# RMSNorm with every row written twice: stores and loads in batches of three and two, wide instructions, gamma spread by a matmul

## The chip, the core and the metric

The kernel runs on one core of a Trainium2 chip. The metric is the device time of one execution in microseconds (us). A core has several engines that work side by side, each through its own instructions in order: TensorE (PE, matrix products), VectorE (DVE), ScalarE (ACT), GpSimd (POOL) and SyncE (SP), which here only issues transfers. Sixteen DMA engines move data between the large memory outside the core (DRAM) and the core's own memory, which has 128 partitions. A second memory on the core, PSUM, also has 128 partitions.

## What is computed

```python
"x": (8, 512, 2048) float32, "gamma": (2048,) float32

x_rep = np.repeat(x, 2, axis=1)
rms = np.sqrt((x_rep ** 2).mean(axis=-1, keepdims=True) + 1e-6)
x_norm = x_rep / rms
return (x_norm * gamma[None, None, :]).astype(np.float32)
```

Each of the 4096 rows of 2048 numbers is divided by its root mean square, multiplied by gamma, and written to the output twice in a row. The input has 33.6 MB, the output 67.1 MB.

## The kernel before

The rows are cut into eight tiles of 512 rows: 128 partitions with four rows each (K = 4). A tile has one buffer `y` of eight rows per partition, as wide as its output. A load (L52) puts the four rows of x into its upper half, rows 4 to 7; the result of row k goes to row 2k and its repetition to row 2k + 1, so that the buffer at the end is the output tile in order and a store (L56) writes it out. Three such buffers take turns (`rows`, bufs=3), so a load of tile i waits until the store of tile i - 3 is complete.

For each row, `square` lets ACT square 2048 numbers into PSUM (`sq`, thrown away) and sum them on the way (L64), then take the root of the mean plus 1e-6 (L68). `scale` takes the reciprocal on DVE (L73) and multiplies the row by it and by gamma in one SCALAR_TENSOR_TENSOR (L74). `repeat` copies the result (L80): on ACT for all rows of a part but the last, where DVE does it. `compute` strings these together so that ACT squares row k + 1 while DVE scales row k.

All loads and stores are issued by SyncE, on one queue, in program order, and SyncE waits at each for what it needs. The order is written by hand (`tc.manual_schedule()`): load 0 in two halves, loads 1 and 2, stores 0 and 1, loads 3 and 4, stores 2 and 3, loads 5 and 6, stores 4 and 5, load 7 in two halves, store 6, and store 7 in two halves. Gamma comes in four pieces to one partition, issued by ACT (L98), and is spread over the partitions by GpSimd (L101) into `gamma_b`. L131 and L142 are the start and end of the launch.

Of the kernel before, what the change touches and what calls it, by code (L numbers as in the profile page):

```python
# [1 line left out]

# [4 lines left out]


@with_exitstack
def kernel(  # L10
    ctx: ExitStack,
    tc: tile.TileContext,
    x: bass.AP,
    gamma: bass.AP,
    out: bass.AP,
):
    nc = tc.nc
    P = nc.NUM_PARTITIONS
    f32 = mybir.dt.float32
    Act = mybir.ActivationFunctionType  # L20
    Alu = mybir.AluOpType

    B, S, D = x.shape
    Bo, So, Do = out.shape
    R = So // S
    assert R == 2 and D == Do and B == Bo and So == S * R
    eps = 1e-6
    inv_d = 1.0 / float(D)


    K = 4
    N = B * S
    assert N % (P * K) == 0
    ntiles = N // (P * K)
    x_t = x.rearrange("b s d -> (b s) d").rearrange("(n p k) d -> n p k d", p=P, k=K)
    out_t = out.rearrange("b s d -> (b s) d").rearrange("(n p j) d -> n p (j d)", p=P, j=K * R)

    singles = ctx.enter_context(tc.tile_pool(name="singles", bufs=1))
    rows = ctx.enter_context(tc.tile_pool(name="rows", bufs=3))
    junk = ctx.enter_context(tc.tile_pool(name="junk", bufs=1, space=bass.MemoryType.PSUM))  # L40
    small = ctx.enter_context(tc.tile_pool(name="small", bufs=8))

    ys = []

    def load(i, eng, parts=1):


        y = rows.tile([P, K * R, D], f32, name="y")
        step = K // parts
        for k in range(0, K, step):  # L50
            at = K * (R - 1) + k
            eng.dma_start(out=y[:, at : at + step, :], in_=x_t[i, :, k : k + step, :])  # L52
        ys.append(y)

    def store(i, k0, k1):
        nc.sync.dma_start(  # L56
            out=out_t[i, :, R * k0 * D : R * k1 * D],
            in_=ys[i][:, R * k0 : R * k1, :].rearrange("p j d -> p (j d)"),
        )

    def square(i, k):
        sq = junk.tile([P, D], f32, name="sq")
        ss = small.tile([P, 1], f32, name="ss")
        nc.scalar.activation(  # L64
            out=sq[:], in_=ys[i][:, K * (R - 1) + k, :], func=Act.Square, accum_out=ss[:]
        )
        rms = small.tile([P, 1], f32, name="rms")
        nc.scalar.activation(out=rms[:], in_=ss[:], func=Act.Sqrt, scale=inv_d, bias=eps_t[:])  # L68
        return rms

    def scale(i, k, rms):
        rstd = small.tile([P, 1], f32, name="rstd")
        nc.vector.reciprocal(out=rstd[:], in_=rms[:])  # L73
        nc.vector.scalar_tensor_tensor(  # L74
            out=ys[i][:, R * k, :], in0=ys[i][:, K * (R - 1) + k, :], scalar=rstd[:], in1=gamma_b[:],
            op0=Alu.mult, op1=Alu.mult,
        )

    def repeat(i, k, copy):
        copy(out=ys[i][:, R * k + 1, :], in_=ys[i][:, R * k, :])  # L80

    def compute(i, k0, k1):

        rms = square(i, k0)
        for k in range(k0, k1):
            scale(i, k, rms)
            if k + 1 < k1:
                rms = square(i, k + 1)
                repeat(i, k, nc.scalar.copy)
            else:  # L90
                repeat(i, k, nc.vector.tensor_copy)


    ctx.enter_context(tc.manual_schedule())
    load(0, nc.sync, parts=2)
    gamma_b = singles.tile([P, D], f32, name="gamma_b")
    for c in range(0, D, D // 4):
        nc.scalar.dma_start(  # L98
            out=gamma_b[0:1, c : c + D // 4], in_=gamma[c : c + D // 4].partition_broadcast(1)
        )  # L100
    nc.gpsimd.partition_broadcast(out_ap=gamma_b[:], in_ap=gamma_b[0:1, :])  # L101
    eps_t = singles.tile([P, 1], f32, name="eps_t")
    nc.vector.memset(eps_t, eps)  # L103
    load(1, nc.sync)
    load(2, nc.sync)

    for i in range(ntiles):
        parts = 2 if i == ntiles - 1 else 1
        for k in range(0, K, K // parts):
            compute(i, k, k + K // parts)  # L110
            store(i, k, k + K // parts)

        if i % 2 == 1:
            for j in (i + 2, i + 3):
                if j < ntiles:
                    load(j, nc.sync, parts=2 if j + 1 == ntiles else 1)


# [1 line left out]
_INS = ['x', 'gamma']  # L120
_OUTS = [((8, 1024, 2048), 'float32')]


# [23 lines left out]
```

## Time and profile before

| | |
|---|---|
| median of 4 runs | 239.87 us (239.53 to 240.31) |
| profiled execution | 239.79 us |
| its span, first to last instruction | 238.0 us |
| DVE busy | 90.8 us (38% of the span), 74 instructions |
| ACT busy | 115.3 us (48%), 121 instructions |
| POOL busy | 2.5 us, 5 instructions |
| loads of 4 MB / 2 MB, issue to landing (median) | 25.1 / 9.6 us |
| stores, issue to landing (median) | 26.8 us (4 MB), 31.6 us (8 MB) |

The groups of instructions that matter, as line, engine, operation, what it writes and reads, shape, count, then busy time and mean duration of one in ns, then the idle time of the engine before them and what ended it:

```profile
L64 ACT ACTIVATE sq<-y 128x2048 f32<-128x2048 f32 x32 | 59.9, 1871 | 84.9 <-DMA y<-in_x_dram 84.9
L74 DVE SCALAR_TENSOR_TENSOR y<-y,rstd,gamma_b 128x2048 f32<-128x2048 f32 x32 | 75.3, 2352 | 1.2 <-DVE rstd L73 0.2
L73 DVE RECIPROCAL rstd<-rms 128x1 f32<-128x1 f32 x32 | 5.2, 162 | 115.7 <-ACT rms L68 115.7
L80 ACT COPY y<-y 128x2048 f32<-128x2048 f32 x23 | 43.4, 1888 | 3.7 <-DVE y L74 3.7
L80 DVE COPY y<-y 128x2048 f32<-128x2048 f32 x9 | 11.0, 1226 | 0.3
L68 ACT ACTIVATE rms<-ss,eps_t 128x1 f32<-128x1 f32 x32 | 9.4, 294 | 1.0
L64 ACT ACTIVATION_READ_ACCUMULATOR sq<-y 128x1 f32 x32 | 6.0, 186 | 0.0
L101 POOL PARTITION_BROADCAST gamma_b<-gamma_b x1 | 2.3, 2292 | 8.4 <-DMA gamma_b<-in_gamma_dram 8.4
```

A long idle time says where an engine waited: ACT waited 84.9 us for loads, DVE 115.7 us for ACT, most of it while ACT itself waited.

### The profile page before, as it was taken

To read this page: it belongs to the slowest core of one execution; us is meant where nothing else is said; L and a number is where in the kernel's file an instruction comes from. 1 tells how busy PE (TensorE), PEld (TensorE's weight loads), DVE (VectorE), ACT (ScalarE), POOL (GpSimd) and SP (SyncE) were. 2 spreads that over 40 slices of the span, in tenths; PEclk is the share of its full clock that TensorE was granted. 3 is DMA by queue.
4 is the path that set the end of the run, shared out by engine and by line. 5 is a ranking of instruction groups with operands and counts; after the bars stand their busy time and mean duration, and the time that the engine had idled before them with its cause. 6 is when DMAs were issued, how large, how long until landed. Compare 5 with 4: busy or idle time off the path is not lost.

```text
span 238.0 us, 301 instructions
## 1 busy us (share of the span) xinstructions
DVE 90.8 (38%) x74; ACT 115.3 (48%) x121; POOL 2.5 (1%) x5
## 2 busy tenths in 40 slices
DVE  0086977864000084967000007696600009900000
ACT  2699999990000299997000049999500049700000
POOL 0300000000000000000000000000000000000000
DMA  7999998989899999989898999989898999999996
GB/s 265 430 452 441 441 441 352 529 352 529 352 424 413 435 419 425 529 352 529 352 529 347 441 430 425 474 374 507 352 529 352 402 435 485 441 419 397 424 441 259
DMA packets 2747, 100.69 MB, mean 423 GB/s; under 512 B 309, under 2 KB 309, under 8 KB 313
## 3 DMA queue, kind: packets, MB, share of 16 engines
q1 hardware_dynamic: 2736, 100.66, 98.7%
q14 instruction: 3, 0.02, 0.0%
q10 hardware_dynamic: 8, 0.01, 0.0%
HBM read 33.56 MB, written 67.11 MB: 423 GB/s over the span
## 4 chain that ended last, share of the span: by engine, by line
DMA 66%; ACT 15%; DVE 6%; issue 1%; SPq 0%; DVEq 0%
DMA out_dram<-y 40%; DMA y<-in_x_dram 25%; ACT sq L64 7%; ACT y L80 5%; DVE y L74 5%; ACT rms L68 1%; ACT L68 1%; DVE y L80 1%; DVE rstd L73 0%; SPq L52 0%; DVEq L74 0%; SPq L56 0%
## 5 line engine op out<-in xcount | busy, mean ns | idle before, releaser
L64 ACT ACTIVATE sq<-y 128x2048 f32<-128x2048 f32 x32 | 59.9, 1871 | 84.9 <-DMA y<-in_x_dram 84.9
L74 DVE SCALAR_TENSOR_TENSOR y<-y,rstd,gamma_b 128x2048 f32<-128x2048 f32 x32 | 75.3, 2352 | 1.2 <-DVE rstd L73 0.2
L73 DVE RECIPROCAL rstd<-rms 128x1 f32<-128x1 f32 x32 | 5.2, 162 | 115.7 <-ACT rms L68 115.7
L80 ACT COPY y<-y 128x2048 f32<-128x2048 f32 x23 | 43.4, 1888 | 3.7 <-DVE y L74 3.7
L80 DVE COPY y<-y 128x2048 f32<-128x2048 f32 x9 | 11.0, 1226 | 0.3
L68 ACT ACTIVATE rms<-ss,eps_t 128x1 f32<-128x1 f32 x32 | 9.4, 294 | 1.0
L64 ACT ACTIVATION_READ_ACCUMULATOR sq<-y 128x1 f32 x32 | 6.0, 186 | 0.0
L101 POOL PARTITION_BROADCAST gamma_b<-gamma_b x1 | 2.3, 2292 | 8.4 <-DMA gamma_b<-in_gamma_dram 8.4
L64 ACT ACT_TABLE_LOAD x1 | 1.3, 1283 | 2.1 <-issue 2.1
L68 ACT ACT_TABLE_LOAD x1 | 1.3, 1283 | 0.0
L103 DVE MEMSET eps_t<- 128x1 f32 x1 | 0.1, 59 | 0.8 <-PEq L131 0.8
L131 POOL MEMSET const-float32-0.0<- 128x1 f32 x1 | 0.1, 100 | 0.2 <-issue 0.2
L131 POOL MEMSET const-bfloat16-1.0<- 128x1 bf16 x1 | 0.1, 102 | 0.0
L131 POOL MEMSET const-uint8-127<- 128x1 uint8 x1 | 0.1, 101 | 0.0
L131 POOL MEMSET const-float32-1.0<- 128x1 f32 x1 | 0.1, 98 | 0.0
## 6 DMA issues: line engine op xcount, KB each, us to landing
y<-in_x_dram SPq DMA_DIRECT2D x6, 4096.0 KB, 25.1
y<-in_x_dram SPq DMA_DIRECT2D x4, 2048.0 KB, 9.6
out_dram<-y SPq DMA_DIRECT2D x2, 4096.0 KB, 26.8
out_dram<-y SPq DMA_DIRECT2D x7, 31.6
gamma_b<-in_gamma_dram ACTq DMA_DIRECT2D x4, 2.0 KB
```

Of the source, the lines that this page charges most:

```text
L64: nc.scalar.activation(out=sq[:], in_=ys[i][:, K * (R - 1) + k, :], func=Act.Square, accum_out=ss[:])
L68: nc.scalar.activation(out=rms[:], in_=ss[:], func=Act.Sqrt, scale=inv_d, bias=eps_t[:])
L73: nc.vector.reciprocal(out=rstd[:], in_=rms[:])
L74: nc.vector.scalar_tensor_tensor(out=ys[i][:, R * k, :], in0=ys[i][:, K * (R - 1) + k, :], scalar=rstd[:], in1=gamma_b[:], op0=Alu.mult, o ...
L80: copy(out=ys[i][:, R * k + 1, :], in_=ys[i][:, R * k, :])
L101: nc.gpsimd.partition_broadcast(out_ap=gamma_b[:], in_ap=gamma_b[0:1, :])
L103: nc.vector.memset(eps_t, eps)
L131: nc = _bacc.Bacc("TRN2", target_bir_lowering=False, num_devices=1)
```

## The change

SyncE's order becomes: the first half of load 0, six pieces of gamma, the second half of load 0, the last piece of gamma, loads 1 and 2, stores 0, 1, 2, loads 3, 4, 5, stores 3 and 4, loads 6 and 7, stores 5, 6, 7. Every store is a whole tile, and so is every load but the first.

Gamma goes to one partition (`gamma_row`). Four matmuls with a row of ones spread it over 128 partitions into PSUM, where `gamma_b` now lies.

The work of a tile is done in wide instructions, and not each tile alike. `by_rows` (tiles 0 and 3) sums each row as before, takes root and reciprocal of two rows at once (`root_quick`), scales row by row and copies several rows in one instruction. `sums` and `mixed` (tiles 1, 2, 4, 6, 7) square the rows from `by_row` on in one ACT instruction, into the still unused rows of the output buffer, and sum them in one DVE reduction (`reduce`); the rows before `by_row` are summed as before. `root` raises the mean plus 1e-6 to the power -0.5 on GpSimd for four rows at once. `mixed` puts the squares of the next tile (`ahead`) before its own scaling. The copies are all on DVE (tiles 0, 4), half on ACT and half on DVE (1, 2, 3, 7), or all on ACT (6). In tile 5 ACT scales by the root, DVE multiplies all four rows by gamma in one instruction, and GpSimd makes the copy. The activation table is loaded ahead of the first load.

```diff
-    def store(i, k0, k1):
+    def load(i, k0, k1):
         nc.sync.dma_start(
+            out=ys[i][:, K * (R - 1) + k0 : K * (R - 1) + k1, :], in_=x_t[i, :, k0:k1, :]
+        )
+    def store(i):
+        nc.sync.dma_start(out=out_t[i], in_=ys[i].rearrange("p j d -> p (j d)"))
+    def total(i, k, ss):
+        sq = junk.tile([P, D], f32, name="sq")
+        nc.scalar.activation(
+            out=sq[:], in_=ys[i][:, x_at + k, :], func=Act.Square, accum_out=ss[:, k : k + 1]
+        )
+    def square(i, k0, k1):
+        nc.scalar.activation(
+            out=ys[i][:, k0:k1, :], in_=ys[i][:, x_at + k0 : x_at + k1, :], func=Act.Square
+        )
+    def reduce(i, k0, k1, ss):
+        nc.vector.tensor_reduce(
+            out=ss[:, k0:k1], in_=ys[i][:, k0:k1, :], op=Alu.add, axis=mybir.AxisListType.X
+        )
+    def root(k0, k1, ss):
+        at = ss[:, k0:k1]
+        nc.gpsimd.tensor_scalar(
+            out=at, in0=at, scalar1=inv_d, scalar2=eps, op0=Alu.mult, op1=Alu.add
+        )
+        nc.gpsimd.tensor_tensor(out=at, in0=at, in1=power_t[:, k0:k1], op=Alu.pow)
...
+    gamma_b = junk.tile([P, D], f32, name="gamma_b")
+    cuts = [0, *range(D // 4, D + 1, D // 8)]
...
+    nc.scalar.preload_act_table(Act.Sqrt)
+    load(0, 0, H)
+    for c0, c1 in zip(cuts[:-2], cuts[1:-1]):
+        gamma_piece(c0, c1)
+    load(0, H, K)
+    gamma_piece(cuts[-2], cuts[-1])
+    bank = 512
+    for c0 in range(0, D, bank):
+        nc.tensor.matmul(
+            gamma_b[:, c0 : c0 + bank], ones[:], gamma_row[:, c0 : c0 + bank], start=True, stop=True
+        )
+    load(1, 0, K)
+    load(2, 0, K)
+    def root_quick(k0, k1, ss):
+        at = ss[:, k0:k1]
+        nc.scalar.activation(out=at, in_=at, func=Act.Sqrt, scale=inv_d, bias=eps_t[:])
+        nc.vector.reciprocal(out=at, in_=at)
+    def by_rows(i, copies):
+        ss = [columns() for _ in range(R)]
+        for h, k0 in enumerate(range(0, K, H)):
+            for k in range(k0, k0 + H):
+                total(i, k, ss[h])
+            root_quick(k0, k0 + H, ss[h])
+            scale(i, k0, k0 + H, ss[h])
+        for k0, k1, copy in copies:
+            repeat(i, k0, k1, copy)
+        store(i)
+    def sums(i, by_row):
+        ss = columns()
+        square(i, by_row, K)
+        for k in range(by_row):
+            total(i, k, ss)
+        return i, by_row, ss
+    def mixed(given, copies, ahead=None):
+        i, by_row, ss = given
+        reduce(i, by_row, K, ss)
+        root(0, K, ss)
+        if ahead is not None:
+            ahead = sums(*ahead)
+        scale(i, 0, K, ss)
+        for k0, k1, copy in copies:
+            repeat(i, k0, k1, copy)
+        store(i)
+        return ahead
+    whole = ((0, K, nc.vector.tensor_copy),)
+    shared = ((0, H, nc.scalar.copy), (H, K, nc.vector.tensor_copy))
+    by_scalar = ((0, H, nc.scalar.copy), (H, K, nc.scalar.copy))
+    by_rows(0, whole)
+    two = mixed(sums(1, 1), shared, ahead=(2, 1))
+    mixed(two, shared)
+    for j in (3, 4, 5):
+        new_tile()
+        load(j, 0, K)
+    by_rows(3, shared)
+    _, _, ss = mixed(sums(4, H), whole, ahead=(5, 0))
+    for j in (6, 7):
+        new_tile()
+        load(j, 0, K)
+    reduce(5, 0, K, ss)
+    root(0, K, ss)
+    for k in range(K):
+        nc.scalar.activation(
+            out=ys[5][:, R * k, :], in_=ys[5][:, x_at + k, :], func=Act.Copy, scale=ss[:, k : k + 1]
+        )
+    y_r = ys[5].rearrange("p (k r) d -> p k r d", r=R)
+    nc.vector.tensor_tensor(
+        out=y_r[:, :, 0, :], in0=y_r[:, :, 0, :],
+        in1=gamma_b[:].rearrange("p (k d) -> p k d", k=1).to_broadcast([P, K, D]), op=Alu.mult,
+    )
+    repeat(5, 0, K, nc.gpsimd.tensor_copy)
+    store(5)
+    last = mixed(sums(6, 1), by_scalar, ahead=(7, 0))
+    mixed(last, shared)
```

`load` of before, with its parts, and the functions `square`, `scale`, `repeat` and `compute` in their old form go. `scale` still multiplies a row by its scalar and gamma, now for rows k0 to k1; `repeat` copies rows k0 to k1 in one instruction.

## The prediction

> **What bounds the kernel now.** I read the page's queue table first, then the stretches, the chain that ended last, and last the timeline of one tile.
>
> ```profile
> q1 hardware_dynamic: 2736, 100.66, 98.7%
> HBM read 33.56 MB, written 67.11 MB: 423 GB/s over the span
> ```
>
> The reader is to see 98.7%: the packets of SyncE's one queue fill 16 DMA engines for all but 3.1 us of the 238.0 us span. The rest is nearly all at the two ends:
>
> ```profile
> core 0: us, DVE busy (x) ACT busy (x) POOL busy (x), PEclk, DMA share, GB/s
> 0.00:2.00 2.00, 0.06 (x1) 0.00 (x0) 0.19 (x4) 1.00 0.52 99
> 2.00:30.00 28.00, 14.40 (x13) 21.99 (x24) 2.29 (x1) 1.00 0.99 424
> 30.00:52.00 22.00, 15.46 (x12) 21.41 (x23) 0.00 (x0) 1.00 1.03 432
> ...
> 236.00:238.00 2.00, 0.00 (x0) 0.00 (x0) 0.00 (x0) 1.00 0.00 0
> ```
>
> A share above 1 only says that packets are long beside a window. DVE and ACT are idle half of the span; what they do matters only if a store is issued too late. The chain confirms it: its long links are transfers.
>
> ```profile
> 26.59 26.02 DMA out_dram<-y
> 52.61 0.02 issue
> 52.63 29.02 DMA y<-in_x_dram
> ...
> 98.67 31.72 DMA out_dram<-y
> ...
> 130.86 38.30 DMA out_dram<-y
> 169.16 0.02 issue
> 169.18 24.22 DMA y<-in_x_dram
> ```
>
> From the trace's packet records I take the prices. A 16 KB packet takes 0.611 us, 32 KB 1.213, 64 KB 2.418, so all data need (512 x 0.611 + 1024 x 1.213 + 896 x 2.418) / 16 = 232.6 us. The first packet starts at 1.74 us, 1.02 after the first issue, and the last ends at 236.80. So 235.1 - 232.6 = 2.5 us is all that any order could win inside. Of these, about 0.7 is the latency of each engine's first packet. The completions (mean over the engines) show the rest: a 4 MB load after a load 9.71 us, an 8 MB store after a store 19.35; a store that a load follows 19.68 and that load 9.36, together the same as unturned; a load that a store follows 9.77 and 9.85, but 10.47 the first time. Turns to stores thus cost some 0.1 us, the first 0.76. The remainder is spread between engines: 1.1 us lie between the first and the last completion of the last store.
>
> **What the Trainium skill says.** "DMA: Bandwidth & Descriptors", "Issuing engines are not separate DMA queues": DMAs of all issuers run on the same 16 engines, so moving gamma's four issues from ACT to SP wins no bandwidth; the trace agrees, with gamma's 84 ns packets between x's. "VectorE: DVE Perf Modes", "The perf-mode tier table": fp32 copies run two elements a cycle, tensor_tensor and tensor_reduce one; the trace agrees for the copy (1226 ns) and shows 2352 ns for the SCALAR_TENSOR_TENSOR; it has no reduce. "GPSIMD Engine Reference", "Performance versus the Vector engine" and "Engine selection": about 2.6 cycles per element at 1.2 GHz for two inputs, one input roughly line rate; no run shown so far has it.
>
> **The change, part by part.**
>
> *Bytes and turns.* The same 100.66 MB. Turns from loads to stores go from four to three, and from stores to loads from three to two: -0.1 to -0.15 us. The last tile whole: 256 load packets become 128, 256 store packets become 128, (256 x 0.611 - 128 x 1.213 + 256 x 1.213 - 128 x 2.418) / 16 = -0.13. Gamma in seven packets on SP's queue, each about 60 to 84 ns, instead of four at 84: up to +0.2 on an engine if all fall on one. SP issues six of them before the second half of tile 0; at 0.21 to 0.51 us each that half is issued near 3.5 us, while the first half's packets last to 7.3: hidden. Sum -0.1, between -0.4 and +0.2.
>
> *Cover of the stores.* Before, stores 1 to 5 wait ready in the queue. Now each is issued shortly before it is needed, so I check all eight. A store must be issued about 1.7 us before the last completion of the transfer ahead: 1.0 from issue to first packet, 0.7 from last packet to completion. Prices: square with sum 2.03 (row 1.87 plus accumulator read); a square or copy of n rows on ACT 0.2 + 1.7 n (from 1.88 for one); DVE copy 0.16 + 1.07 n (from 1.226); SCALAR_TENSOR_TENSOR 2.36, taken unchanged with gamma in PSUM, between -0.1 and +0.1; reduce, at one element per cycle, 0.1 + 2.13 n (estimate, VectorE page). R is the root on GpSimd (two instructions of four columns and two handovers): a four-column job above its 0.1 us MEMSETs, between 0.5 and 3.5, I take 1.2. Each store's readiness:
>
> Store 0: gamma's last piece lands near 13.3 (its packet behind the second half, 12.2, plus the 1 us that gamma's packets took to complete); four matmuls, no row in the trace, 0.4 to 2 us, taken as 1.5: 14.8. Two rows 4.7, reciprocal 0.2, two rows 4.7, copy of four 4.4: 28.9. Deadline 33.3 - 1.7 = 31.6.
> Store 1: 28.9 + 6.5 + R + 9.4 + 2.3 = 47.1 + R; deadline 52.6 - 1.7 = 50.9.
> Store 2: one more tile, 65.4 + 2R; deadline 70.2. The next tile's squares run on ACT beside this.
> Loads 3, 4, 5 are issued behind it at 68, 72 and 92 us, each with a transfer still running.
> Store 3: load 3 completes near 101.0; two squares 4.1, root 0.5, four rows 9.6, copy of two 2.3: 117.4. Deadline 120.5 - 1.7 = 118.8.
> Store 4: ACT is free of tile 3 at 113.9, square of two rows 3.6, reduce 4.4, R, 9.4, copy 4.4: 135.7 + R; deadline 138.2.
> Store 5: reduce 8.6, R, four scaled copies on ACT 7.6, a multiply of 8192 columns 8.7, then the GpSimd copy P: 160.6 + 2R + P. Deadline 178.7 - 1.7 = 177.0. P from the GPSIMD page is 8192 columns at 1.03 to 2.6 cycles, 7.0 to 17.8 us (estimate); I take 9.
> Store 6: load 6 at 168.9, 5.3 + 6.5 + R + 9.4 + 3.6: 193.7 + R; deadline 196.4. Its root stands behind P on GpSimd, free at 172.0, before the reduce ends at 180.7.
> Store 7: 210.5 + 2R; deadline 215.8.
>
> So no queue runs dry if R stays under 2.4 and P under 14; the least spare, at R = 1.2, is about 1.3 us, at stores 3 and 4. If cover fails, the missing time is added whole to the end.
>
> *Removed work.* The partition broadcast (2.29 us), the second table load (1.28), and most of the 32 roots and reciprocals all lay beside transfers: nothing. The early table load is likewise beside the first transfer.
>
> Sum against the profiled execution: 239.79 - 0.1 = 239.7; it lies 0.08 below the median 239.87. I take 239.6, since a little of the spread between engines may go with the fewer turns.
>
> **Rivals.**
>
> *A. The turns cost more than their own rows show* (chance 0.20). The spread between engines grows from 0.4 us at load 0 to 1.1 at the end, and steps up at turns; with fewer of them, and the 0.76 at the first store gone, the end comes 1.2 us earlier: 238.6. Against: that 0.76 may belong to the first store, which remains.
>
> *B. The root on GpSimd is slow and the stores come late* (0.29). DVE waits for R with nothing else queued that could start: in tile 2, scale, copy and store stand behind it. SyncE's queue is in order too, so loads 3 to 5 wait behind store 2. It decides from R = 2.4. At R = 2.9 store 2 is 1.0 late; measured from the slipped loads, store 4 is 0.4 late, store 6 0.2 and store 7 0.3: +1.9, 241.5. For it: five tiles carry it, and no row of before bounds it. Against: MEMSETs of 0.1 us.
>
> *C. The GpSimd copy of tile 5 outlasts its cover* (0.10). At the two-input price, P = 17.8, store 5 comes 3.8 us late: 243.4. Against: it has one input.
>
> **How the numbers follow.** The forecast, covered stores and 239.6, has 0.41; its own range is 239.1 to 240.2. About 0.2%, 0.48 us, is what a measurement can tell from no change, so the forecast gives about 0.09 to faster and 0.32 to same; A gives all to faster (0.29), B and C to slower (0.39). The range takes in A and B and leaves out most of C and the strongest of B: 238.4 to 242.0.
>
> **What would show it.** Right: DMA share of q1 stays near 98.7%, each store's issue is before the completion of the transfer ahead, GpSimd's pow rows are near 1 us with their handover. Wrong: a stretch of low DMA share just ahead of stores 2, 3, 4, 5 or 6, with the chain passing through DVE, POOL or ACT there; B if DVE waits over 2.4 us for POOL, C if the chain runs through the POOL copy. If the span falls by more than 0.5 us with no idle stretch, the turns (A) were worth more than their rows.

## The result, and the profile after

| | before | after |
|---|---|---|
| median of the runs | 240.05 us (62 runs, 239.53 to 241.39) | 240.72 us (44 runs, 239.22 to 241.31) |
| ratio, with its 95% interval | | 1.0025 (1.0018 to 1.0032) |
| profiled execution / its span | 239.79 / 238.0 us | 241.0 / 239.2 us |

The change makes the kernel slower by 0.25%, some 0.6 us. The forecast was 239.6 us, a little faster than before. The time lies inside the whole range (238.4 to 242.0), but outside the forecast's own (239.1 to 240.2), and on the other side of no change.

First the page of the kernel after: its span, its queue, and the groups of instructions whose price the prediction had to guess (columns as before).

```profile
span 239.2 us, 245 instructions
...
q1 hardware_dynamic: 2462, 100.67, 98.1%
HBM read 33.56 MB, written 67.11 MB: 421 GB/s over the span
...
L87 DVE SCALAR_TENSOR_TENSOR y<-y,ss,gamma_b 128x2048 f32<-128x2048 f32 x28 | 64.7, 2345 | 10.4 <-POOL ss L83 7.3
L74 DVE TENSOR_REDUCE ss<-y 128x3 f32<-128x6144 f32 (+2 forms) x6 | 41.4, 6903 | 11.2 <-ACT y L69 11.2
L80 POOL TENSOR_SCALAR ss<-ss 128x4 f32<-128x4 f32 x6 | 1.2, 193 | 169.2 <-DVE ss L74 169.2
L94 POOL COPY y<-y 128x8192 f32<-128x8192 f32 x1 | 7.0, 7009 | 16.6 <-DVE y L194 16.6
L127 PE MATMUL gamma_b<-gamma_row,ones 1*128 1x512 f32 x8 | 7.2, 1079 | 8.1 <-DMA gamma_row<-in_gamma_dram 8.1
L83 POOL TENSOR_TENSOR ss<-ss,power_t 128x4 f32<-128x4 f32 x6 | 6.1, 1008 | 0.5
```

The queue's packets fill 98.1% of 239.2 us, which is 234.7 us per DMA engine; before it was 98.7% of 238.0, or 234.9. So the packets took as long in sum as they did, and the extra time of this execution lies around them. Fewer instructions run (on ACT 47 for 121), and most of the engines' own times are near what was assumed: the root is two instructions of 0.19 and 1.01 us, GpSimd's copy 7.0. The matmuls are the exception, 7.2 us where 1.5 was taken.

When SyncE issued its transfers, from the timeline of the kernel after (start, time until the last of the group is issued, both in us, then what was issued and how many):

```profile
8.30 0.83 SPq L51 DMA_DIRECT2D y<-in_x_dram  x2
29.31 39.43 SPq L56 DMA_DIRECT2D out_dram<-y  x3
68.83 22.34 SPq L51 DMA_DIRECT2D y<-in_x_dram  x3
116.93 19.97 SPq L56 DMA_DIRECT2D out_dram<-y  x2
139.19 20.12 SPq L51 DMA_DIRECT2D y<-in_x_dram  x2
170.13 43.37 SPq L56 DMA_DIRECT2D out_dram<-y  x3
```

Stores 0 to 2 begin to be issued at 29.31 us, stores 3 and 4 at 116.93, stores 5 to 7 at 170.13. Loads 2, 5 and 7, which run ahead of these three, completed at 32.15, 119.43 and 178.45 (mean over the 16 DMA engines, from the trace's completion records). The queue never ran dry.

The completion records say where the 0.6 us are. Two traces of each kernel, all in us:

| | before | before again | after | after again |
|---|---|---|---|---|
| load 2, time after the load ahead of it | 10.47 | 10.61 | 9.72 | 9.74 |
| load 7, the same (before: its two halves added) | 9.56 | 9.55 | 10.51 | 10.50 |
| mean over the engines, last completion | 236.54 | 236.47 | 236.44 | 236.71 |
| last engine behind this mean | 0.58 | 0.65 | 1.59 | 0.65 |
| from there to the end of the span | 0.89 | 0.90 | 1.18 | 1.19 |
| span | 238.01 | 238.02 | 239.21 | 238.55 |

A load after a load takes 9.71. Against that, load 2 had lost 0.75 to 0.9 before and loses nothing now, and load 7 loses 0.8 now. So the mean end stands still (236.5 and 236.6). What is added is an engine that ends further behind the others (0.5 on the average of two and two, but anything from nothing to 1.0) and 0.3 us between the last completion and the end of the span.

### The profile page after: what moved, and what is told of

Read it like the earlier page. It is cut to its first block, busy times and chain, and to the rows that moved or that the text cites. A ratio compares the mean times of both kernels' runs of the same rounds, so it can differ in the third digit from the quotient of the medians.

```text
span 239.2 us, 245 instructions
## 1 busy us (share of the span) xinstructions
PE 7.2 (3%) x8; PEld 2.3 (1%) x8; DVE 132.9 (56%) x45; ACT 90.7 (38%) x47; POOL 14.7 (6%) x20
## 3 DMA queue, kind: packets, MB, share of 16 engines
q1 hardware_dynamic: 2462, 100.67, 98.1%
## 5 line engine op out<-in xcount | busy, mean ns | idle before, releaser
L87 DVE SCALAR_TENSOR_TENSOR y<-y,ss,gamma_b 128x2048 f32<-128x2048 f32 x28 | 64.7, 2345 | 10.4 <-POOL ss L83 7.3
L74 DVE TENSOR_REDUCE ss<-y 128x3 f32<-128x6144 f32 (+2 forms) x6 | 41.4, 6903 | 11.2 <-ACT y L69 11.2
L69 ACT ACTIVATE y<-y 128x6144 f32<-128x6144 f32 (+2 forms) x6 | 33.6, 5604 | 26.4 <-DMA y<-in_x_dram 26.4
L63 ACT ACTIVATE sq<-y 128x2048 f32<-128x2048 f32 x13 | 24.4, 1874 | 42.2 <-DMA y<-in_x_dram 42.1
L94 ACT COPY y<-y 128x4096 f32<-128x4096 f32 x6 | 21.6, 3604 | 30.7 <-DVE y L87 30.7
L94 DVE COPY y<-y 128x4096 f32<-128x4096 f32 (+1 forms) x6 | 18.0, 3004 | 0.2
L190 ACT ACTIVATE y<-y,ss 128x2048 f32<-128x2048 f32 x4 | 7.8, 1994 | 18.8 <-POOL ss L83 18.8
L194 DVE TENSOR_TENSOR y<-y,gamma_b 128x8192 f32<-128x8192 f32 x1 | 8.7, 8689 | 9.3 <-ACT y L190 9.3
L94 POOL COPY y<-y 128x8192 f32<-128x8192 f32 x1 | 7.0, 7009 | 16.6 <-DVE y L194 16.6
L127 PE MATMUL gamma_b<-gamma_row,ones 1*128 1x512 f32 x8 | 7.2, 1079 | 8.1 <-DMA gamma_row<-in_gamma_dram 8.1
```

Source lines behind the costliest of these rows:

```text
L63: nc.scalar.activation(out=sq[:], in_=ys[i][:, x_at + k, :], func=Act.Square, accum_out=ss[:, k : k + 1])
L69: nc.scalar.activation(out=ys[i][:, k0:k1, :], in_=ys[i][:, x_at + k0 : x_at + k1, :], func=Act.Square)
L74: nc.vector.tensor_reduce(out=ss[:, k0:k1], in_=ys[i][:, k0:k1, :], op=Alu.add, axis=mybir.AxisListType.X)
L87: nc.vector.scalar_tensor_tensor(out=ys[i][:, R * k, :], in0=ys[i][:, x_at + k, :], scalar=rstd[:, k : k + 1], in1=gamma_b[:], op0=Alu.mul ...
L94: copy(out=y_r[:, k0:k1, 1, :], in_=y_r[:, k0:k1, 0, :])
L127: nc.tensor.matmul(gamma_b[:, c0 : c0 + bank], ones[:], gamma_row[:, c0 : c0 + bank], start=True, stop=True)
```

## The experiments

What had to be explained: why load 2 was cheap and load 7 dear now, whether the order of the transfers, gamma's path or the wide instructions brought the time, and why one engine ended late. A "turn" below is a load with a store behind it in the queue; the "lead" of a turn is how long before that load's mean completion the store was issued. Theories have letters, which are not those of the prediction's rivals: A, B and C are stated in the first expectation, D and E with the late store 5, F and G with the added instructions on DVE.

**The order alone.** The kernel before with only the new sequence of loads and stores; the last tile is still in halves, gamma and the instructions are the old ones.

```diff
-        if i % 2 == 1:
-            for j in (i + 2, i + 3):
-                if j < ntiles:
-                    load(j, nc.sync, parts=2 if j + 1 == ntiles else 1)
+        for j in {2: (3, 4, 5), 4: (6, 7)}.get(i, ()):
+            load(j, nc.sync, parts=2 if j + 1 == ntiles else 1)
```

> The kernel before with the new sequence of loads and stores alone (3 stores, 3 loads, 2 stores, 2 loads, 3 stores); rows, gamma and the two halves of the last tile as before, so that every store is ready early. Theory A (the batched sequence itself costs the time): 240.6 to 240.8 us, ratio 1.002 to 1.003 against before. Theory B (gamma's seven pieces in SyncE's queue make one DMA engine late): within 0.1% of before, or 0.1 us faster by the missing pair of turns. Theory C (stores issued just in time, by the wide instructions): within 0.1% of before too.

Measured: 240.28 us (21 runs), ratio 1.0021 (1.0012 to 1.0030). Fewer turns alone make it slower, about as much as the whole change does. Its timeline of issues:

```profile
26.63 29.91 SPq L56 DMA_DIRECT2D out_dram<-y  x3
56.64 35.37 SPq L52 DMA_DIRECT2D y<-in_x_dram  x3
118.08 15.13 SPq L56 DMA_DIRECT2D out_dram<-y  x2
140.49 20.05 SPq L52 DMA_DIRECT2D y<-in_x_dram  x3
160.65 39.25 SPq L56 DMA_DIRECT2D out_dram<-y  x4
```

Store 0 (26.63) and store 5 (160.65) stand ready long before the loads ahead of them complete (33.11 and 179.33); store 3 (118.08) only 2.2 us before. Load 2 took 10.70 and the second half of load 7 5.62 where the first half took 4.89, while load 5 took 9.71. Two turns are dear, 1.0 and 0.7, and both are those with an early store. Theory A's time came, but these two turns are a narrower cause than the order as a whole, and the later runs test it.

**Gamma alone.** The kernel before with gamma in seven pieces on SyncE's queue and the matmul into PSUM; nothing else.

```diff
-    for c in range(0, D, D // 4):
-        nc.scalar.dma_start(
...
-    nc.gpsimd.partition_broadcast(out_ap=gamma_b[:], in_ap=gamma_b[0:1, :])
+    for c0, c1 in zip(cuts[:-2], cuts[1:-1]):
+        gamma_piece(c0, c1)
...
+    for c0 in range(0, D, bank):
+        nc.tensor.matmul(
+            gamma_b[:, c0 : c0 + bank], ones[:], gamma_row[:, c0 : c0 + bank], start=True, stop=True
+        )
```

> The kernel before with the new gamma alone: seven pieces on SyncE's queue, spread by a matmul with ones into PSUM. Theory A: within 0.1% of before. Theory B: ratio about 1.002, and the DMA engine that carries the pieces is the last to finish, 0.3 to 0.5 us behind the others' mean more than before. Theory C: within 0.1% of before.

Measured: 240.2 us, ratio 1.0009 (0.9998 to 1.0019), which can't be told from no change. One of the 14 executions took 254.3 us and is not in the ratio; it happens to be the profiled one. Its timeline:

```profile
8.05 21.64 PE L115 MATMUL gamma_b<-gamma_row,ones 1*128 1x512 f32 x8 [8.05 <-DMA gamma_row<-in_gamma_dram]
...
44.16 0.35 SPq L56 DMA_DIRECT2D out_dram<-y  x1
```

The eight matmuls took 21.6 us in place of 7.2, so gamma was ready at 29.7 and store 0 went out at 44.16: some 14 us were lost at the start. Why they were slow once does not show. No other execution with the matmul came out some 14 us late.

**The change with the old gamma.** The kernel after, with gamma in four pieces issued by ACT and spread by GpSimd.

```diff
-    for c0, c1 in zip(cuts[:-2], cuts[1:-1]):
-        gamma_piece(c0, c1)
...
+    for c in range(0, D, D // 4):
+        nc.scalar.dma_start(
+            out=gamma_b[0:1, c : c + D // 4], in_=gamma[c : c + D // 4].partition_broadcast(1)
+        )
+    nc.gpsimd.partition_broadcast(out_ap=gamma_b[:], in_ap=gamma_b[0:1, :])
...
```

> The changed kernel with gamma as before (four pieces issued by ScalarE, spread by GpSimd). Theory A: stays at 240.6 to 240.8. Theory B: falls to 240.0 or below. Theory C: stays at 240.6 to 240.8.

Measured: 242.82 us (4 runs), ratio 1.0126 (1.0112 to 1.0139), over 2 us slower than with the matmul. None of theories A, B and C expected that. Gamma is ready earlier and store 0 goes out at 26.90 in place of 29.31. Load 2 then takes 10.81, 1.1 more than in after, and every load behind it is late. Stores 3 and 4 come at 118.98 and 138.61, only 1.6 and 1.4 us before the completion of the transfer ahead of them, and nine and twelve of the 16 DMA engines ran dry for 0.1 to 0.3 us there. The mean end is 2.1 us later (238.52); what load 2 doesn't explain was lost mostly at store 4 and load 6 (20.20 and 9.83 against 19.74 and 9.44). An earlier gamma, and with it an earlier store 0, made the kernel slower.

**The work of after in the order of before.** Stores and loads two and two, but the wide instructions and the new gamma.

```diff
-    mixed(two, shared)
-    for j in (3, 4, 5):
+    for j in (3, 4):
...
+    mixed(two, shared)
...
     store(5)
+    new_tile()
+    load(7, 0, K)
```

> The changed kernel with the old sequence of loads and stores (2 stores, 2 loads, ...; the last tile undivided): stores 2 to 5 are then ready before the loads ahead of them have landed. Theory A: falls to about 240.0. Theory B: stays at 240.6 to 240.8. Theory C: falls, to about 240.0, since most stores are issued early again.

Measured: 269.54 us (4 runs), ratio 1.1235 (1.1220 to 1.1249). Two lines of its windows (the stretch, its length, the busy time and count of PE, weight loads, DVE, ACT and POOL, then PEclk, DMA share and GB/s):

```profile
160.00:176.00 16.00, 0.00 (x0) 0.00 (x0) 10.91 (x2) 12.13 (x6) 2.16 (x1) 1.00 0.45 197
176.00:180.00 4.00, 0.00 (x0) 0.00 (x0) 4.00 (x1) 0.00 (x0) 4.00 (x1) 1.00 0.00 0
```

and of its timeline:

```profile
165.09 8.69 DVE L194 TENSOR_TENSOR y<-y,gamma_b 128x8192 f32<-128x8192 f32 x1 [9.26 <-ACT y L190]
173.84 7.01 POOL L94 COPY y<-y 128x8192 f32<-128x8192 f32 x1 [16.64 <-DVE y L194]
180.87 0.34 SPq L56 DMA_DIRECT2D out_dram<-y  x1
...
181.27 0.42 SPq L51 DMA_DIRECT2D y<-in_x_dram  x1
212.40 7.03 ACT L69 ACTIVATE y<-y 128x8192 f32<-128x8192 f32 x1 [40.24 <-DMA y<-in_x_dram]
```

No theory expected that. The DMA engines stand still from 168 us on: tile 5 goes through ACT, DVE and GpSimd one after the other, store 5 waits for that, and load 7 is queued behind store 5. Load 7 then lands so late (212.40) that store 6, whose copies stand behind tile 7's squares on ACT, comes late too (226.46). Tile 5's work in three wide steps needs transfers to hide behind that the old order doesn't give. So the parts can't be priced one by one and added: the wide work is cheap only with the new order.

**Store 5 later.** The question was whether load 7 is dear because store 5 was issued 8.3 us ahead (theory D), or for another reason. GpSimd makes three of its four copies once more, and nothing else changes.

```diff
+    repeat(5, 0, K - 1, nc.gpsimd.tensor_copy)
     repeat(5, 0, K, nc.gpsimd.tensor_copy)
```

> The changed kernel, with GpSimd copying three rows of tile 5 once more before the full copy (the output is the same), so that store 5 is issued about 5.3 us later, near 175.4 us, some 2 us ahead of the end of load 7 instead of 7. Theory D (a store that waits in the ring for more than about 4 us behind a load in flight stretches the load's last packets by 0.8 us on every engine, one issued 2 us ahead does not): load 7 takes 9.7 to 9.8 us again instead of 10.5, and the time falls by 0.8 us, ratio to before 0.999 to 1.000. Theory E (each turn to stores costs 0 to 0.9 us by chance, whatever the issue time): no change on the mean, ratio 1.002 to 1.003.

Measured: 239.59 us (14 runs), ratio to before 0.9989 (0.9975 to 1.0003). The kernel after stands at 1.0025, so 5.4 us more work took some 0.9 us away. The timeline of after around it, then that of this kernel:

```profile
163.09 7.01 POOL L94 COPY y<-y 128x8192 f32<-128x8192 f32 x1 [16.64 <-DVE y L194]
...
170.13 0.34 SPq L56 DMA_DIRECT2D out_dram<-y  x1
...
180.04 7.03 ACT L69 ACTIVATE y<-y 128x8192 f32<-128x8192 f32 x1 [3.94 <-DMA y<-in_x_dram]
```

```profile
163.13 12.38 POOL L94 COPY y<-y 128x6144 f32<-128x6144 f32 x2 [16.64 <-DVE y L194]
...
175.54 0.34 SPq L56 DMA_DIRECT2D out_dram<-y  x1
...
179.41 7.03 ACT L69 ACTIVATE y<-y 128x8192 f32<-128x8192 f32 x1 [3.20 <-DMA y<-in_x_dram]
```

ACT starts on tile 7 when load 7 has landed on every engine: at 180.04 with the store issued at 170.13, at 179.41 with the store issued at 175.54. The load's own step fell from 10.51 to 9.79, and the mean end from 236.4 to 235.75. The last engine was still 1.65 us behind that mean, so the late engine is another matter.

**Store 0 later in the kernel before.** The same test at the other dear turn: the last copy of tile 0 is made three times.

```diff
-                repeat(i, k, nc.vector.tensor_copy)
+                for _ in range(3 if i == 0 else 1):
+                    repeat(i, k, nc.vector.tensor_copy)
```

> The kernel before, with VectorE making the copy of the last row of tile 0 three times (the output is the same), so that store 0 is issued about 2.4 us later, near 29.0 us, some 2 us ahead of the end of load 2. Theory D: load 2 takes 9.7 us instead of 10.5, and the time falls by 0.8 us, ratio 0.9965. Theory E: within 0.1% of before.

Measured: 240.05 us (14 runs), ratio 1.0007 (0.9993 to 1.0021): no gain. The timeline shows the store where it was wanted:

```profile
25.21 3.75 DVE L80 COPY y<-y 128x2048 f32<-128x2048 f32 x3
...
29.03 0.35 SPq L56 DMA_DIRECT2D out_dram<-y  x1
```

Load 2 fell from 10.47 to 9.72, as expected. But load 4, at the next turn, rose from 9.77 to 10.32, and the mean end stayed at 236.4. In the kernel before, the stores of the later turns are issued 18 us ahead and cost only 0.06 to 0.16. Once the first turn is free, the second pays most of its price. So not every early store is dear: the first is, or the one after a turn whose store came late.

**Second traces of both kernels.** Nothing is changed; they are the columns "again" above.

> The changed kernel once more, for a second trace. Theory D: load 2 again 9.7 us and load 7 again 10.5 us, the other turns under 0.3 us. Theory E: the dear turn lies elsewhere. If the one engine that finished 1.6 us behind the mean is a property of the program, it is there again; if it is chance, the last completion lies 0.4 to 1.2 us behind the mean.

> The kernel before once more, for a second trace. Theory D: load 2 again 10.5 us, the other loads at turns under 10.0. Theory E: the dear turn lies elsewhere, or there are two or none.

The price of load 7 (10.51, 10.50), that of load 2 in before (10.47, 10.61) and the closing stretch (1.18, 1.19 against 0.89, 0.90) repeat. The late engine of after does not: 1.59, then 0.65.

**All stores late, in narrow instructions.** If the lead decides, the order of the first experiment should gain once its stores 0 and 5 are late too. The last copy of tile 0 is made three times; the last copy and the store of tile 5 are put behind the first scaling of tile 6.

```diff
+            if k == k0 and between is not None:
+                between()
...
-                repeat(i, k, nc.vector.tensor_copy)
+                for _ in range(last):
+                    repeat(i, k, nc.vector.tensor_copy)
+
+    def finish():
+        repeat(5, K - 1, nc.vector.tensor_copy)
+        store(5, 0, K)
...
+            compute(
+                i, k, k + K // parts, last={0: 3, 5: 0}.get(i, 1), between=finish if i == 6 else None
+            )
```

> The new sequence with the rows, gamma and halves of before (as in the run of the sequence alone), and two stores issued late: VectorE makes the last copy of tile 0 three times, and the last copy of tile 5 only after it has scaled the first row of tile 6 (the output is the same). Each of the three turns to stores then has a store issued about 3 us ahead. Theory D: no load takes over 9.9 us at a turn, the completions' mean ends 0.8 us earlier than before's 236.5, and the time is about 239.1, ratio 0.996 to 0.997. Theory E: 240.3 as the sequence alone, ratio 1.002. If the late engine of the changed kernel comes from the sequence, the last completion is again 1.5 us behind the mean in some executions; if from gamma or the wide instructions, it stays under 0.9.

Measured: 239.11 us (6 runs, 239.02 to 239.70), ratio 0.9968 (0.9956 to 0.9980): it beats both kernels, and the order alone by 1.2 us. Its issues, from the timeline:

```profile
28.97 29.61 SPq L56 DMA_DIRECT2D out_dram<-y  x3
58.69 32.41 SPq L52 DMA_DIRECT2D y<-in_x_dram  x3
117.31 15.13 SPq L56 DMA_DIRECT2D out_dram<-y  x2
139.68 20.04 SPq L52 DMA_DIRECT2D y<-in_x_dram  x3
174.69 24.46 SPq L56 DMA_DIRECT2D out_dram<-y  x4
```

Beside the order alone, 26.63 has become 28.97 and 160.65 has become 174.69. The loads ahead took 9.74, 9.71 and, in halves, 4.89 and 4.90. No turn is dear, and the mean end is 235.78 against 237.37. The page shows the same in its packets:

```profile
q1 hardware_dynamic: 2736, 100.66, 98.6%
```

Of 237.4 us that is 234.1 per DMA engine; for the order alone it is 98.5% of 239.2, or 235.6. There is no matmul in it and no wide instruction. So the order as such doesn't cost the time (theory A). Its last engine was 0.77 us behind.

**More instructions on DVE.** The closing stretch was 0.28 longer in after. In the traces DVE's last drain began 0.54 us after its release there and 0.11 in before. Whether that follows from the small number of instructions was tried with 64 one-column MEMSETs on DVE while it waits for load 3.

```diff
+    pad_t = singles.tile([P, 1], f32, name="pad_t")
+    for _ in range(64):
+        nc.vector.memset(pad_t, 0.0)
     by_rows(3, shared)
```

> The changed kernel with 64 MEMSETs of one column more on VectorE while it waits for load 3 (the output is the same). Theory F (the closing barrier is 0.3 us longer [...]a matter of how many it has had): the time from the last completion to the end of the span falls from 1.17 to about 0.9 us, and the time by 0.3. Theory G (the longer close comes from TensorE or GpSimd taking part): it stays at 1.17.

Measured: 240.84 us (6 runs), ratio 1.0043 (1.0027 to 1.0058). In the profiled execution the stretch was 0.83 in place of 1.18, and DVE's drain began 0.11 us after its release again. The stretch depends on DVE's instructions, though not on their number alone: the change with the old gamma has the 45 of after, and its drain came after 0.11 too. The stretch is a part of the span, but the median isn't lower than that of after, so that it adds to the time isn't shown; six executions from 240.13 to 241.64 us are too few for 0.3.

**Gamma back on ACT's queue, the matmul kept.** ACT issues gamma in four pieces, behind both halves of load 0. This asks whether the small gamma packets between the loads are what makes one engine late (theory B), and it makes store 0 early again.

```diff
-        nc.sync.dma_start(out=gamma_row[:, c0:c1], in_=gamma[c0:c1].partition_broadcast(1))
+        nc.scalar.dma_start(out=gamma_row[:, c0:c1], in_=gamma[c0:c1].partition_broadcast(1))
...
```

> The changed kernel with gamma's row in four pieces issued by ScalarE as before, still spread by the matmul. Theory B (gamma's pieces in SyncE's queue make one engine late): the last completion lies under 0.8 us behind the mean, and the time falls by about 0.3 us to 240.3. If the queue of the pieces does not matter: 240.5 to 240.8, as the changed kernel.

Measured: 242.08 us (6 runs), ratio 1.0075 (1.0052 to 1.0098), some 1.2 us slower than after by the two ratios. The timeline of after, then of this kernel:

```profile
24.85 4.43 DVE L94 COPY y<-y 128x8192 f32<-128x8192 f32 x1
...
29.31 0.35 SPq L56 DMA_DIRECT2D out_dram<-y  x1
...
32.55 5.32 ACT L69 ACTIVATE y<-y 128x6144 f32<-128x6144 f32 x1 [2.53 <-DMA y<-in_x_dram]
```

```profile
22.28 4.43 DVE L94 COPY y<-y 128x8192 f32<-128x8192 f32 x1
...
26.74 0.35 SPq L56 DMA_DIRECT2D out_dram<-y  x1
...
33.33 5.32 ACT L69 ACTIVATE y<-y 128x6144 f32<-128x6144 f32 x1 [3.49 <-DMA y<-in_x_dram]
```

Store 0 goes out 2.6 us earlier and load 2 lands 0.8 later (its step 10.61 against 9.72). The last engine was 2.0 us behind, more than in after, with no gamma packet on SyncE's queue; so gamma's packets there are not what makes it late (theory B).

**Both edits.** The late store 5 and the 64 MEMSETs together.

> The changed kernel with store 5 late and with the 64 MEMSETs, both as above. Theory D and theory F together: 0.3 us below the run with store 5 late alone (239.59), near 239.3, ratio 0.997 to 0.998; mean of the last completions 235.7, close 0.85 us. What is left over the run of the sequence with late stores (239.11) is then the engine that lags: if that comes with the wide instructions, some executions stand 0.8 to 1.5 us above the fastest; if it was chance, they lie within 0.7 us as there.

Measured: 239.42 us (15 runs), ratio 0.9976 (0.9960 to 0.9992). This is the change itself with no dear turn, and it beats before. The last of its groups of stores goes out where it was wanted:

```profile
175.67 37.88 SPq L56 DMA_DIRECT2D out_dram<-y  x3
```

The loads at its turns took 9.73, 9.72 and 9.76. Against the late store 5 alone the MEMSETs brought nothing that can be told from noise (the intervals overlap). The executions lie between 238.78 and 240.62. Those of the narrow order with late stores lie within 0.7 us, but they are only six, and before with store 0 late, narrow too, has 239.39 to 241.24. So the scatter doesn't tell whether the late engine comes with the wide work.

All turns together, each as lead and step of the load ahead, in us (a load after a load takes 9.71; "h" marks half a load, 4.88 undisturbed; the second traces give the same within 0.2):

| kernel | first turn | second | third | fourth |
|---|---|---|---|---|
| before | 6.4: 10.47 | 18.4: 9.77 | 18.4: 9.85 | 26.1: 5.02 h |
| before, store 0 late | 3.1: 9.72 | 19.1: 10.32 | 18.6: 9.86 | 26.1: 5.01 h |
| order alone | 6.5: 10.70 | 2.2: 9.71 | 18.7: 5.62 h | |
| order alone, stores 0 and 5 late | 3.2: 9.74 | 2.2: 9.71 | 3.1: 4.90 h | |
| after | 2.8: 9.72 | 2.5: 9.71 | 8.3: 10.51 | |
| after, store 5 late | 2.9: 9.73 | 2.5: 9.71 | 2.3: 9.79 | |
| after, gamma on ACT's queue | 6.3: 10.61 | 2.7: 9.71 | 8.4: 10.33 | |
| after, old gamma | 6.6: 10.81 | 1.6: 9.71 | 8.3: 10.41 | |
| after, MEMSETs | 3.0: 9.73 | 2.4: 9.72 | 8.3: 10.51 | |
| after, store 5 late and MEMSETs | 2.9: 9.73 | 2.4: 9.72 | 2.2: 9.76 | |
| after, order of before (up to the standstill) | 2.8: 9.71 | 19.0: 10.22 | 18.2: 9.75 | |
| before, new gamma (the execution of 254.3 us) | store behind the load: 9.71 | 19.9: 10.89 | 18.6: 9.77 | 26.1: 4.92 h |

Every turn with a lead of 3.2 us or less is free. With 6.3 or more a turn is dear (0.5 to 1.2) if it is the first of its kernel or follows a free one, and nearly free (0.04 to 0.15) if it follows another early store. Leads between 3.2 and 6.3 were not tried. What happens in a queue that holds the next store early is not seen in the records, which show only longer packets at the end of the load. That remains a pattern, tested in both directions, without a mechanism. It speaks for theory D, with this exception, and against C, which blamed the stores issued just in time, and E, which left it to chance.

## Why the prediction was wrong, and where it was right

**Stores and their deadlines: right.** The prediction's stores were ready at 28.9, 48.3, 67.8, 117.4, 136.9, 172.0, 194.9 and 212.9; they were issued at 29.31, 48.89, 68.40, 116.93, 136.56, 170.13, 195.19 and 213.16. The limits were set a little too early: from the last packet of a load to its completion the records of before have 0.3 to 0.5 us, not 0.7, which only a store ahead of a load needs. Rival B fell: DVE waited 1.5 us for the root, not over 2.4. Rival C fell: the copy took 7.0 us, not over 14. What the Trainium skill says of one-input work in "GPSIMD Engine Reference", "Engine selection" (roughly line rate) holds for this copy: the lower of the prediction's two bounds was the true one. Gamma was ready at 15.37 (14.8 was taken), since most of the matmuls' 7.2 us passed before its last piece came; it made store 0 0.4 us later, without loss, since that store's limit was 31.6.

**Bytes and turns: the step that failed.** The prediction held that a turn has a price of its own, some 0.1, so that three turns cost less than four, and left the 0.76 of load 2 with "the first store, which remains". The runs show that this price is set by when the store is issued and by the turn before it. Gamma's later arrival moved store 0 from 26.59 to 29.31, and load 2 became free. Store 5, ready 8.3 us ahead, made load 7 dear. What one gained the other took: the mean end of the engines moved by +0.1 instead of the -0.1 to -0.3 of the sum. That the two nearly cancel is luck. The prediction asked of each store only whether it came too late; it never asked whether it came too early.

**Rival A: a real gain that this change doesn't get.** A gave 238.6 if the dear turn went and the turns were worth more than their rows. The dear turn at load 2 did go. The order with all its stores late reached 239.11, the change with store 5 late 239.59, and with the MEMSETs too 239.42. So the gain was there, and the change threw it away at one store. The spread between engines, which A let shrink with the turns, did not shrink.

**The spread between engines: mis-sized.** It was taken as not growing, perhaps shrinking. The last engine ended 1.59 and 0.65 us behind the mean in after, 0.58 and 0.65 in before. The jump comes at loads 6 and 7, behind the turn from store 4. In the first trace of after the late engine had one packet of store 4 that took 3.38 us instead of 2.42, and two of 1.69 and 2.24 instead of 1.21 at the end of load 7. Its size changes from one execution to the next (0.65 to 2.0 in the kernels with wide instructions whose queue didn't stand still, 0.6 to 1.0 in the narrow ones). Gamma's packets on SyncE's queue are ruled out as its cause; what makes it was not found. A kernel with wide instructions and half loads at the end, or other sizes of packets, was not tried.

**The end of the span: a term that was missing.** Between the last completion and the end lie 1.18 us in after and 0.89 in before. The sum had no such term. It is in both profiled executions of after. Whether it is a part of the 0.6 us between the medians stays open, since the MEMSETs that removed it from the trace did not lower the median.

**The sum.** On the average of the two traces each: mean end +0.1, last engine +0.5, closing stretch +0.3, together +0.9 for profiled executions of 241.0 and 240.33 against 239.79 twice; the medians differ by 0.67. So the time that was added lies in the last two terms, as far as two traces of each can say, and the gain that should have outweighed it was lost at load 7. Without the dear load 7 the mean end would be 0.7 to 0.8 lower and the change a gain, which is what the last experiment measured. The prediction gave a slower time 0.39, but by rivals B and C. Both fell, so the slower time came in a way that none of its rivals named.

**Removed work: right.** The order with late stores keeps the old broadcast, roots and reciprocals and was no slower (239.11) than the change with late stores (239.42), so removing them was worth nothing, as forecast. The matmul brought a rare risk that the prediction didn't name, eight matmuls of 2.7 us in one execution of fourteen.

## What to carry to other kernels

In a kernel bound by one queue of loads and stores, check each store against two limits: late enough that it isn't issued long before the load ahead is done, early enough that no engine runs dry. Here a store issued 2 to 3 us before the load's completion cost nothing, one issued 6 us or more ahead could cost 0.5 to 1.2 us, and at 1.6 and 1.4 us engines ran dry for 0.1 to 0.3. Make all of them late: with only the first made late, the price moved to the next turn. A change whose work is all hidden still moves the moments at which transfers are issued, and at this level (a few tenths of a per cent) these moments are the change.

## What was not expected of the hardware

- Work that was put in ahead of a store made the kernel faster: 5.4 us more of GpSimd took 0.9 us away, and the order alone gained 1.2 us from its two stores being late.
- The same bytes took medians from 239.1 to 242.8 us where no engine ran dry for more than 0.3 us. Their packets took 234.1 us per DMA engine in the fastest of these kernels (98.6% of 237.4) and 236.4 in the slowest (98.2% of 240.7).
- Four fp32 matmuls of 1x512 show as eight of 1079 ns. In one execution they took 2.7 us each, at a granted clock of 1.00.
- The stretch from the last completion to the end of the span was 0.3 us shorter in the profiled executions with 64 more short instructions on DVE (0.83 against 1.18 us).
